# A streaming encoder layer on one core: the order of the in-projection blocks, and weight preparation without a limit on VectorE's backlog

## The chip, the cores and the metric

The kernel runs on one core of a Trainium2 chip. The metric is the device time of one execution in microseconds (us); less is better. The kernel uses TensorE (PE, with its weight loads PEld), VectorE (DVE), ScalarE (ACT), GpSimd (POOL), and the DMA queues of SyncE (SP), POOL and ACT.

## The reference, cut to what matters

One layer processes 1024 rows of a prompt and 64 rows of a running stream, 1088 in all, with 2048 features each.

```
h = rms_norm(x, norm_g)
z = h @ w_in                              # 2048 x 7296: 57 blocks of 128 columns
u, v, g_a = split(z[:, :3072], 3)         # part A
vn = layer_norm(gelu(v), ...)
out_a = gelu(u) * sgu_mix(vn) * silu(g_a)
r, k, vb, hw, ha = split(token_shift(z[:, 3072:6272]), ...)   # part B
d = w0 + tanh(hw) @ w2 ;  decay = exp(-exp(-softplus(-d) - 0.5)) ;  a = sigmoid(a0 + ha @ a2)
# per head, per row: S = S * decay - (S kk) b^T + v k^T ;  y = S r     (16 heads of 64)
out_b = (group_norm(y) * gn_g + gn_b + bonus) * silu(z[:, 6272:])
y = rms_norm(x + concat(out_a, out_b) @ w_out, final_g)
```

The outputs are y for both streams, the last states S, the last unshifted rows, and vn of the short stream.

## The kernel before, in words

**Blocks.** The in-projection is cut into 57 blocks of 128 output columns. Blocks 0 to 7 are u, 8 to 15 v, 16 to 23 the gate g_a, 24 to 31 r, 32 to 39 k, 40 to 47 vb, 48 holds hw and ha, and 49 to 56 are the gates of part B. Activations `h` and weights are each split into a high and a low part of 16 bits, and three products (high by high, high by low, low by high: `PASSES`) are added in PSUM. A block is three groups of columns (364, 364 and 360 rows of h, `MG`), each with 16 x 3 matrix products (`in_group`, L569). `h` fills the large tile `bigt` until the last block has run.

**Weights.** For each block or out-projection group a generator `wprep` (L535) takes raw weights from one tile `raw`. It squares them on ACT, sums them with a small product on PE (`total`), derives a power-of-two scale on DVE, and then splits four pieces of 512 columns: the high part on ACT, the low part on DVE (L194). After that it issues the load of the next raw weights on SP's queue. The preparation of job i + 1 is added to the planner when job i starts on PE.

**Part B by pairs.** Two heads make a pair; pair q needs k block 32 + q, vb block 40 + q, r block 24 + q, and at its end gate 49 + q. A finished k, vb or r block is written to DRAM by `z_out` (L626), a gate by `gate_out` (L635), both on SP's queue, and their u buffer is then free. `front(q)` (L825) computes decay and a, reads k, then the state and r, and then vb (`z_load`, L643), all on SP's queue, and multiplies on POOL, ACT and DVE. It then writes the tiles AR and KB in three parts; a part waits for the flags "mid", "late" and "chain" of pair q - 1. `wkv(q)` (L928) forms products of these parts, masks them on POOL (L1022), and transposes KB on PE (after which the flag ("kbfree", q) is set). It then inverts a triangular system: four DVE transposes (L1045), thirty steps of two DVE instructions (L1049 to L1056), a second set of transposes, and small products on PE. After it comes a chain of 17 steps, each of which goes from PE to DVE and back; its end stores the state `o_sp` (L1167). `front(q + 1)` is added right after the first four transposes of `wkv(q)`. `post(q)` (L1197) does the group norm, multiplies by the gate and writes the mix row block to DRAM. `a_out(i)` (L737) does the same for part A from blocks i and 16 + i, with two POOL instructions among others.

**Out-projection.** It has two halves of the contracted dimension, each with eight groups of 256 output columns. Half 0 needs mixes 0 to 6 and 8 (pair 0), half 1 the rest (`HALF`). `mix_prep(0)` (L1248) is added when block 31 is done. It waits for its mixes, computes a scale, waits for ("kbfree", 7), and then starts `mix_stage`, which reads the eight tiles back on POOL's queue. Each tile is split into two halves of 16 bits in two pieces, high part on ACT and low part on DVE (L1274). Tiles 0 and 1 go to part of `wk`. For tiles 2 to 7, `mix_place` (L1282) takes a u buffer if `room7` allows it, and else waits until the in-projection has ended and takes a place in `bigt`; such tiles are later moved to u buffers by `mix_move`. `out_first` (L1355) runs group 0 of half 0: for four row blocks at a time it first takes tiles 0 to 5, then 6 and 7.

**Buffers.** There are 13 u buffers of 128 x 1105 floats. Every in-projection block takes one, and so do most steps of `front`, `wkv`, `post` and `a_out`. `room7` (L1235) counts how many must stay free for work still to come before a mixed tile may take one.

**The planner.** The order of instructions on each engine is fixed when the program is built. `run` issues the matrix products of the blocks in the order of `order`, and after every few products calls `poll` (L155). It holds an estimated clock for each engine, and advances every generator whose due time has come. A generator is passed over while the estimated clock of DVE is ahead of PE's by more than the generator's `backlog` (ns):

```
for it in list(self.side):
    if it[0] > self.now or self.clk[DV] > self.now + it[2]:
        continue
```

The engines then run their streams on the chip in that order, and semaphores make one wait for another. DMA queues issue in order too.

Of the kernel before, what the change touches and what calls it, by code (L numbers as in the profile page):

```python
# [44 lines left out]
class Builder:  # L45
# [1188 lines left out]

    def room7(self, staging=False):  # L1235
        F = self.flags
        need = 0 if ("gb", 7) in F else 1
        if ("mix", 7) not in F:
            need += (23 not in self.gelu_buf) + (7 not in self.fbuf)
        if staging:  # L1240
            pass
        elif ("xal", 7) not in F:
            need += 4
        elif ("xfr", 7) in F and ("ysq", 7) not in F:
            need += 3
        return len(self.ufree) > need
# [242 lines left out]
    def run(self):  # L1489
        nc = self.nc  # L1490
        order = list(range(8, 16)) + [48, 32, 40, 24]
        for q in range(7):
            order += [49 + q, q, 16 + q]
            if q < 6:
                order += [33 + q, 41 + q, 25 + q]
        order += [39, 47, 31, 7, 23, 56]
        jobs = [("in", b) for b in order] + [("out", hf, g) for hf in range(2) for g in (0, 1, 2, 3, 4, 5, 7, 6)]
        self.jobs = jobs
        self.mstg = {}
        self.mixT = [{}, {}]  # L1500
        self.mixA, self.mixB = [], []
        self.minv = [None, None]
        gen = lambda i: self.wprep(jobs[i], i, jobs[i + 1] if i + 1 < len(jobs) - 2 else None)
        self.late = order[:3]
        self.raws = {}
        self.xarr = {}
        self.xf, self.xp = {}, {}
        self.load_consts()
        for j in range(2):
            self.xarr[0] = self.dma(nc.sync, self.xw[0][:, j * 1024:(j + 1) * 1024],  # L1510
                                    self.a["x"][0:128, j * 1024:(j + 1) * 1024], 1 << 19)
        self.raw_load(jobs[0])
        self.x_load(1)
        self.raw_load(jobs[1], [self.alloc(), self.alloc()])
        self.x_load(2)
        self.raw_load(jobs[2], [self.alloc(), self.alloc()])
        self.x_load(3)
        self.load_consts2()
        self.add(self.startup(), front=True)
        self.add(self.after_x())  # L1520
        plan = [(0, 0, 128), (0, 128, 128), (1, 0, 256), (0, 256, 128), (2, 0, 256), (1, 256, 128), (2, 256, 128)]
        plan += [(i, 384, 128) for i in range(3)]
        plan += [(i, t0, 128) for t0 in (512, 640) for i in range(3)]
        plan += [(i, t0, n) for i in range(3) for t0, n in ((768, 256), (1024, 64))]
        for i, t0, n in plan:
            while ("x", (t0 + n + 127) // 128 - 1) not in self.flags or ("w", jobs[i]) not in self.flags:
                self.spin()
            self.in_group(order[i], i, t0, n)
            if t0 == 1024:
                self.block_done(order[i])  # L1530
                if i == 0:
                    self.add(gen(3), backlog=2500)
        nj = len(jobs)
        for i, job in enumerate(jobs):
            if i < 3 or i > nj - 3:
                continue
            while ("w", job) not in self.flags:
                self.spin()
            if i < nj - 3:
                self.add(gen(i + 1), backlog=2500)  # L1540
            if i == nj - 6:
                self.add(self.raw_late(jobs[-2:]))
            if i == nj - 5:
                self.add(gen(nj - 2), backlog=2500)
            if job[0] == "in":
                b = job[1]
                if b == 32:
                    self.add(self.front(0), backlog=1e9)
                if b < 8:
                    self.add(self.a_load(b))  # L1550
                for t0, n in MG:
                    self.in_group(b, self.wset(i), t0, n)
                self.block_done(b)
                if b == 31:
                    self.add(self.mix_prep(0, None), backlog=1e9)
                if jobs[i + 1][0] == "out":
                    self.flags.add("inproj")
                    self.add(self.mix_move(), backlog=1e9)
            else:
                hf, gi = job[1], job[2]  # L1560
                if hf == 0 and gi == 0:
                    self.out_first(self.wset(i))
                    self.add(self.mix_prep(1, [self.wk[:, j * NT:(j + 1) * NT].bitcast(F16) for j in range(8)]))
                    continue
                if hf == 1 and gi == 0:
                    self.free(*self.mixA)
                    self.add(self.fg_load())
                if i < nj - 3:
                    self.out_group(hf, gi, self.wset(i))
                else:  # L1570
                    self.add(gen(nj - 1), backlog=2500)
                    self.out_last([(jobs[k][2], self.wset(k)) for k in range(nj - 3, nj)])
        nc.scalar.dma_start(self.a["o_sh"], self.sh[:].rearrange("p a b -> p (a b)"))
        while self.side:
            self.spin()
# [70 lines left out]
```

## Time and profile before

| | us |
|---|---|
| three runs: median (lowest to highest) | 1996.18 (1995.94 to 1999.48) |
| the profiled execution, its own time | 1999.07 |
| its span, first to last instruction | 1997.4 |
| mean granted clock of TensorE | 0.988 of full |

The profiled execution is one execution of the same program; its time lies 2.9 us above the median of the three runs. Its trace gives the start and duration of every instruction. "Busy" is time in which an engine executes; idle time is put down to what ended it. The granted clock is a share of 2.4 GHz; where it is not 1.0, part of the stretch ran at 1.2 GHz. A row of the timeline merges neighbouring instructions of the same kind ("x4").

### The profile page before, as it was taken

The numbers are of one execution on the slowest core, as the hardware profiler recorded it, in microseconds if no ns is written. First come the engines' busy times: TensorE is split into PE (matmuls) and PEld (weight loads), VectorE is DVE, ScalarE is ACT, GpSimd is POOL, SyncE is SP. The second block draws the span as 40 slices with busy tenths as digits, with TensorE's granted clock in tenths as the row PEclk, the third lists the DMA queues.
The fourth block names the chain that finished last, engine by engine and source line by source line (L and its number), as shares of the span: only waits on it lengthen the run. The fifth ranks groups of instructions, "written<-read, shape, count | busy, mean of one in ns | idle before, by whom it ended". The sixth has DMA issues, their size and how long they took to land. (4 is left out here: it accounts for less than half of the span.)

```text
span 1997.4 us, 42939 instructions
## 1 busy us (share of the span) xinstructions
PE 1929.3 (97%) x18429; PEld 1395.4 (70%) x18429; DVE 1152.4 (58%) x2557; ACT 1017.8 (51%) x1855; POOL 351.9 (18%) x360
## 2 busy tenths in 40 slices
PE   6999999999999999999999999999999789999998
PEld 6966667665766666676666666666666468899997
DVE  6574684274566557548456654753845676553444
ACT  7633334566556555654755565565473633232433
POOL 2400000330420240141033034005102400100000
PEclk9999999999999999999999999999999889999999
DMA  6221123222222312211232131221132344512114
GB/s 237 86 75 43 46 97 139 100 79 67 89 69 84 138 43 86 108 63 62 100 122 66 61 142 64 82 101 69 67 133 77 145 143 162 199 58 100 68 41 141
DMA packets 52622, 192.33 MB, mean 96 GB/s; under 512 B 6928, under 2 KB 18720, under 8 KB 42768
## 3 DMA queue, kind: packets, MB, share of 16 engines
q1 hardware_dynamic: 42064, 157.33, 22.7%
q0 software_dynamic: 6880, 22.26, 3.2%
q10 hardware_dynamic: 3488, 9.99, 1.3%
q8 instruction: 145, 2.38, 0.5%
q14 instruction: 45, 0.37, 0.1%
HBM read 140.32 MB, written 45.93 MB: 93 GB/s over the span
## 5 line engine op out<-in xcount | busy, mean ns | idle before, releaser
L245 PE MATMUL mp<-bigt,w 128*128 128x364 f16 (+3 forms) x8508 | 1330.3, 310 | 2.0 <-DVE w L194 1.1
L245 PEld LDWEIGHTS <-w 128*128 128x128 f16 x9216 | 816.8, 98 | 409.3 <-issue 4.5
L194 DVE SCALAR_TENSOR_TENSOR w<-raw,sci,w 128x512 f16<-128x512 f32 x276 | 231.7, 863 | 179.3 <-ACT w L186 178.7
L245 PEld LDWEIGHTS <-wk 128*128 128x128 f16 x2304 | 209.8, 98 | 35.8 <-ACT wk L186 3.7
L186 ACT ACTIVATE w<-raw,sci 128x512 f16<-128x512 f32 x276 | 185.9, 714 | 57.5 <-DVE sci L303 50.0
L245 PE MATMUL mp<-w,wk 128*128 128x256 f16 x1728 | 204.8, 274 | 9.5 <-DVE bigt L194 6.0
L201 POOL TENSOR_TENSOR u<-u,u 128x544 f32<-128x544 f32 (+1 forms) x112 | 152.1, 1387 | 274.1 <-DVE u L194 82.5
L186 ACT ACTIVATE w<-raw 128x2048 bf16<-128x2048 f32 (+1 forms) x70 | 131.8, 1883 | 96.2 <-PE mp L245 95.6
L186 ACT ACTIVATE wk<-bigp 128x512 f32<-128x512 f32 (+6 forms) x248 | 120.8, 511 | 69.7 <-PE bigp L245 37.3
L186 ACT ACTIVATE u<-yps 64x128 f32<-64x128 f32 x120 | 32.8, 273 | 220.9 <-DVE wk L203 220.3
L245 PE MATMUL mp<-w,u 128*128 128x256 f16 x1035 | 127.9, 273 | 0.0
L186 ACT ACTIVATE u<-mp,sc 128x364 f32<-128x364 f32 (+3 forms) x109 | 57.2, 524 | 133.9 <-PE mp L245 132.8
L194 DVE SCALAR_TENSOR_TENSOR bigt<-mp,sc,bigt 128x512 f32<-128x512 f32 (+2 forms) x83 | 53.9, 652 | 109.2 <-PE mp L245 108.9
L1131 DVE SCALAR_TENSOR_TENSOR S<-S,pc,smp 64x64 f32<-64x64 f32 x240 | 66.9, 279 | 80.0 <-PE smp L245 76.3
L186 ACT ACT_TABLE_LOAD x84 | 107.8, 1283 | 7.6 <-PE smp L245 3.2
L245 PEld LDWEIGHTS <-u 128*128 128x128 f16 x1035 | 100.6, 98 | 12.0
L186 ACT ACTIVATE u<-mp,zs 128x364 f32<-128x364 f32 (+1 forms) x75 | 42.0, 560 | 128.7 <-PE mp L245 128.4
L203 POOL TENSOR_TENSOR wk<-wk,mask 128x512 f32<-128x512 f32 (+1 forms) x80 | 85.1, 1084 | 121.0 <-ACT wk L186 117.5
L203 DVE TENSOR_TENSOR u<-u,u 128x228 f32<-128x228 f32 (+15 forms) x248 | 90.8, 367 | 8.3
L194 DVE SCALAR_TENSOR_TENSOR u<-mp,zs,u 128x363 f32<-128x363 f32 (+1 forms) x100 | 49.4, 494 | 77.2 <-ACT sht L186 52.3
L203 DVE TENSOR_TENSOR u<-bigp,u 128x512 f32<-128x512 f32 (+3 forms) x72 | 41.6, 579 | 80.8 <-PE smp L245 55.5
L223 DVE STREAM_TRANSPOSE wk<-u 32x256 f32<-32x256 f32 (+1 forms) x128 | 57.9, 453 | 45.4 <-ACT u L186 43.6
(186 smaller groups left out, 1912.0 us busy)
## 6 DMA issues: line engine op xcount, KB each, us to landing
raw<-w_in SPq DMA_DIRECT2D x54, 1024.0 KB, 4.9
raw<-w_out SPq DMA_DIRECT2D x14, 1024.0 KB, 4.9
z_d<-u SPq DMA_DIRECT2D x24, 544.0 KB, 4.1
u<-z_d SPq DMA_DIRECT2D x24, 544.0 KB, 5.0
mix_d<-u ACTq DMA_DIRECT2D x16, 544.0 KB, 3.0
o_y<-bigt SPq DMA_DIRECT2D x16, 512.0 KB, 4.1
wk<-x SPq DMA_DIRECT2D x7, 1024.0 KB, 7.9
bigt<-x POOLq DMA_DIRECT2D x7, 1024.0 KB, 9.0
```

What stands on the lines that cost most here:

```text
L186: self.nc.scalar.activation(out, in_, func, bias=bias, scale=scale, **kw)
L194: self.nc.vector.scalar_tensor_tensor(out, in0, s, in1, op0, op1)
L201: eng.tensor_tensor(out[:, c], a[:, c], b[:, c], op)
L203: (eng or self.nc.vector).tensor_tensor(out, a, b, op)
L223: self.nc.vector.transpose(out, a)
L245: self.nc.tensor.matmul(out, lhsT, rhs, start=start, stop=stop)
L1131: self.nc.vector.scalar_tensor_tensor(Sn[hp, hp], Sc[hp, hp], pc[hp, c - 1:c], pu[hp, hp], ALU.mult, ALU.add)
```

## The change

The order of the in-projection blocks is rewritten. Before, the blocks after 8 to 15, 48, 32, 40 and 24 were groups of gate 49 + q, u block q, g_a block 16 + q, then k, vb and r of pair q + 1, for q from 0 to 6 (the last group without k, vb, r), and then 39, 47, 31, 7, 23, 56. After, the first group has no gate (0, 16, 33, 41, 25), each later group q begins with gate 48 + q, the groups run on through pair 7's k, vb and r (54, 6, 22, 39, 47, 31), and the list ends with 7, 23, 55, 56. So the k, vb and r blocks of pairs 1 to 7 and all u and g_a blocks stand one place earlier, gates 49 to 54 five places later, gate 55 seven places later, and gate 56 where it was.

`room7` counts a free buffer for each of the last two gates that is neither done nor holding its buffer; before it counted one for the last gate until it was done.

The weight preparations added in the loop over jobs get a backlog limit of 1e9 ns instead of 2500, so that `poll` never passes them over for DVE's clock. The preparations of job 3 and of the last two jobs keep 2500.

```diff
     def room7(self, staging=False):
         F = self.flags
-        need = 0 if ("gb", 7) in F else 1
+        need = sum(1 for b in (6, 7) if ("gb", b) not in F and 49 + b not in self.gelu_buf)
         if ("mix", 7) not in F:
             need += (23 not in self.gelu_buf) + (7 not in self.fbuf)
...
         order = list(range(8, 16)) + [48, 32, 40, 24]
         for q in range(7):
-            order += [49 + q, q, 16 + q]
-            if q < 6:
-                order += [33 + q, 41 + q, 25 + q]
-        order += [39, 47, 31, 7, 23, 56]
+            order += [48 + q, q, 16 + q] if q else [0, 16]
+            order += [33 + q, 41 + q, 25 + q]
+        order += [7, 23, 55, 56]
...
             if i < nj - 3:
-                self.add(gen(i + 1), backlog=2500)
+                self.add(gen(i + 1), backlog=1e9)
```

## Rows read from the trace of the kernel before

**Rows 1.** The page: busy time by engine, granted clock of 40 slices, weight-splitting group.

```profile
PE 1929.3 (97%) x18429; PEld 1395.4 (70%) x18429; DVE 1152.4 (58%) x2557; ACT 1017.8 (51%) x1855; POOL 351.9 (18%) x360
...
PEclk9999999999999999999999999999999889999999
...
L194 DVE SCALAR_TENSOR_TENSOR w<-raw,sci,w 128x512 f16<-128x512 f32 x276 | 231.7, 863 | 179.3 <-ACT w L186 178.7
```

**Rows 2.** Windows: stretch, length, busy time per engine, granted clock, DMA share, GB/s.

```profile
60.00:1560.00 1500.00, 1478.22 (x13365) 999.63 (x13364) 878.29 (x2011) 812.26 (x1430) 302.95 (x293) 1.00 0.25 84
1560.00:1589.00 29.00, 23.75 (x274) 15.48 (x272) 18.91 (x13) 11.93 (x26) 13.97 (x19) 0.88 0.43 148
1589.00:1610.00 21.00, 9.39 (x49) 5.28 (x50) 18.59 (x44) 14.88 (x23) 1.67 (x3) 0.67 0.79 290
1610.00:1632.00 22.00, 18.86 (x194) 16.22 (x191) 20.65 (x48) 0.00 (x0) 0.00 (x0) 0.92 0.51 176
```

**Rows 3.** Waits of PE, 1589 to 1660: releaser, total us, times, longest us.

```profile
PE mp L245 <- DVE bigt L194: 12.7, 7, 3.1
PE mp L245 <- DVE wk L194: 2.0, 2, 1.5
PE mp L245 <- ACT wk L186: 1.6, 2, 1.1
PE smp L245 <- ACT w L186: 1.4, 1, 1.4
```

**Rows 4.** Timeline of PE: start, us, instruction, count, idle before it.

```profile
1569.93 1.12 PE L250 MATMUL bigp<-ident,wk 128*128 128x128 f32 x4 [5.19 <-ACT wk L186]
...
1589.45 0.39 PE L245 MATMUL mp<-w,wk 128*128 128x256 f16 x2 [0.51 <-ACT wk L186]
...
1618.54 1.44 PE L245 MATMUL mp<-w,wk 128*128 128x256 f16 x6 [3.14 <-DVE bigt L194]
```

**Rows 5.** Timeline of POOL: state stores, the run before 1566, first staging into bigt.

```profile
560.85 1.10 POOL L1168 DMA_DIRECT2D o_sp<-S  x2 [4.22 <-DVE wk L219]
...
1375.76 1.10 POOL L1168 DMA_DIRECT2D o_sp<-S  x2 [5.20 <-DVE S L211]
...
1556.49 2.64 POOL L201 TENSOR_TENSOR u<-u,u 128x544 f32<-128x544 f32 x2
...
1564.56 1.03 POOL L203 TENSOR_TENSOR wk<-wk,pc 128x512 f32<-128x512 f32 x1
...
1582.16 0.54 POOL L253 DMA_DIRECT2D bigt<-mix_d  x1 [0.74 <-PE mp L245]
```

**Rows 6.** Timeline of DVE: transposes of the inverse, one long split, mix splits.

```profile
420.85 3.93 DVE L223 STREAM_TRANSPOSE u<-wk 32x1024 f32<-32x1024 f32 x2
...
571.15 1.96 DVE L223 STREAM_TRANSPOSE u<-wk 32x1024 f32<-32x1024 f32 x1
...
1405.20 1.99 DVE L223 STREAM_TRANSPOSE u<-wk 32x1024 f32<-32x1024 f32 x1
...
1556.68 9.47 DVE L194 SCALAR_TENSOR_TENSOR w<-raw,sci,w 128x512 f16<-128x512 f32 x1 [0.85 <-ACT w L186]
...
1581.00 1.96 DVE L223 STREAM_TRANSPOSE u<-wk 32x1024 f32<-32x1024 f32 x1
...
1604.30 2.87 DVE L194 SCALAR_TENSOR_TENSOR bigt<-bigt,pwi 128x544 f16<-128x544 f32 x4
...
1627.32 1.97 DVE L223 STREAM_TRANSPOSE u<-u 128x1024 f32<-128x1024 f32 x1
```

**Rows 7.** Timeline of SP's DMA queue in pair 6: issue time, issue duration.

```profile
1349.48 0.32 SPq L253 DMA_DIRECT2D g_d<-u  x1
...
1351.34 0.47 SPq L253 DMA_DIRECT2D u<-z_d  x1
1361.98 0.34 SPq L253 DMA_DIRECT2D raw<-w_in  x1
1362.36 0.43 SPq L253 DMA_DIRECT2D u<-z_d  x1
```

## The prediction

> **What bounds the kernel now.** I read the page first. TensorE (PE) is busy for 97% of the span, VectorE (DVE) for 58% and ScalarE (ACT) for 51%; of the forty slices only 33 and 34 show a granted clock under nine tenths [rows 1]. So the end is set by the sum of PE's work, and a change can only give back time in which PE stands still or runs at the lower of its two clock levels (1.2 instead of 2.4 GHz). Then I asked for windows. From 60 to 1560 us PE is idle for 21.8 us of 1500. Slices 33 and 34 hold the change from in-projection to out-projection: 11.6 us idle of 21 (1589 to 1610) and 3.1 of 22 (1610 to 1632) [rows 2]. The waits of PE from 1589 to 1660 name the cause: 12.7 of 17.7 us are waits for DVE to write a `bigt` tile, 3.6 us for the `wk` tiles of the same kind [rows 3]. These are the tiles of the mixed activations that `mix_prep` scales and splits in two for the first out-projection half. In order of time, PE starts its first out-projection product at 1589.45 and meets its longest hole, 3.14 us, at 1618.54; another hole of 5.19 us stands before, at 1569.93 [rows 4].
>
> Why are these tiles late? `mix_prep` may start only when pair 7 has freed its `KB` region ("kbfree"), and the staging DMAs on POOL's queue reach the `bigt` buffers from 1582.16, six microseconds before the in-projection ends [rows 5]. At the same time DVE does pair 7's triangular inverse, which begins with the transposes at 1581.00 and is closed by those from 1627.32 on, so near 1631 [rows 6]; DVE is busy 18.6 of 21 and 20.7 of 22 us [rows 2]. The sixteen splitting instructions (2.87 us for four, so 11.5 us in all [rows 6]) queue between the steps of the inverse.
>
> **What sets when pair 7 comes.** I take the first transpose of each inverse as the mark of a pair. In the trace each inverse opens with four of these, and rows 6 show the first of pairs 0, 1, 6 and 7. From pair 0 to pair 1 it takes 571.15 - 420.85 = 150.3 us, from there to pair 6 (1405.20) 834.1 us in five steps, 166.8 us each [rows 6]. The mark of pair 1 follows the state store of pair 0's chain (`o_sp`, 560.85) by 10.3 us, that of pair 6 the store of pair 5's chain (1375.76) by 29.4 us [rows 5, 6]. So in the later pairs the work before the mark waits for something else than the chain. The DMA queue of SP shows for what: pair 6's `r` is read back at 1351.34, right behind the write of a gate (1349.48), and `v` at 1362.36, right behind a load of raw weights (1361.98) [rows 7]. The queue issues in order, and the gate's write waits until the gate's block has left PE. The recurrence is thus tied to the blocks: six blocks per pair, 166.8 / 6 = 27.8 us per block with the recurrence's work in between.
>
> **The order of blocks.** All blocks from 0 on move one place earlier, except the gates; within a group of six the order is as before. The k, v, r blocks of pairs 1 to 7, and the gate behind which `r` queues, come one block earlier. The work of PE, the copies and the DMAs are the same in number: removed 0, added 0. Pair 0 depends on blocks 48, 32, 40 and 24, which keep their places. Its successor cannot profit at once, since pair 1 came 10.3 us behind the chain already; I take its mark as unmoved, 571. Where the ties come 27.8 us earlier and the own pace is 150.3 against 166.8 us, each pair regains up to 16.5 us, so by pair 3 the recurrence is tied again, one block earlier. Pair 7's mark is then expected near 1581.00 - 27.8 = 1553, while the in-projection ends where it did, since PE's work before it hardly changes. The mixes 0 to 6 and 8 that `mix_prep` needs, and its trigger (block 31), also come one block earlier.
>
> From 1553 to 1589 DVE has 36 us. The inverse alone needs some 35 (1631 less 1581, less the 11.5 us of splitting and one weight preparation of 3.5), two weight preparations take four splits of 0.863 us each [rows 1], so 6.9, and the splitting 11.5: it does not all fit, but only the splitting is due by 1589, and `mix_prep` is not held back by DVE's queue. The other limit is room: h still occupies `bigt`, and six of eight tiles need one of 13 u buffers. `room7` now also counts gate 6 until its buffer is taken, one more than before; but pair 7's four buffers are then already taken and no longer reserved. I expect four of the six to fit early. The other two are split while PE works through the first six tiles of the first four row blocks. Waits left in 1589 to 1660: about 5 us, for `out_add` and the rest. Bounds: 0 (all 17.7 go) and 17.7 (nothing does). I take 12.7 us off.
>
> The clock: 0.67 of full over 21 us and 0.92 over 22 us are, at two levels, 13.9 and 3.5 us at half clock [rows 2]. With PE's busy share in each window (0.45 and 0.86) this is 6.2 + 3.0 = 9.2 us of busy time at half speed, 4.6 us lost. The lowered clock stands in the same windows as the holes; without holes I give back 4.0, bounds 0 and 4.6.
>
> The hole at 1569.93 comes from one DVE instruction, a weight split of 9.47 us from 1556.68 [rows 6], whose span lies under POOL's unbroken run from 1556.49 to 1565.6 (rows 5 show the first and the last of its five rows). ACT, then PE, wait behind it: 5.2 us [rows 4], and some us more for a half-clock stretch around it: 0.88 over 29 us is 7 us at half clock [rows 2]; at PE's busy share of 0.82 that would lose 2.9, but the hole lies in it, so I take 2.1. POOL's run is `a_out(7)` and pair 7's masks; both move by one block, so the meeting may recur. Bounds 0 and 7.3 us; I take the middle, 3.6, since which DVE instruction meets that run is open.
>
> **Weight preparation without the backlog limit.** Before, a step of `wprep` was emitted only when the planner saw DVE's queue under 2.5 us. Nothing is added; steps are emitted earlier. Between 1589 and 1660 PE has no row of waiting for a `w` tile from DVE [rows 3], so there is nothing to gain on PE; raw loads may leave SP earlier, by which `v` would come earlier. Against it, four splits per block can now stand ahead of recurrence steps in DVE's queue, 3.5 us per block [rows 1]. The chain steps of 1500 us cost PE at most the 21.8 us idle of that window [rows 2]. Bounds: a quarter of it goes (5 us gain) or it grows by half (11 us loss); I take 2 us loss, since PE has other products between the chain's steps to hide the rest.
>
> The page "SBUF — State Buffer" of the Trainium skill, section "Who interferes with whom", says that a DVE instruction with two SBUF inputs and a GpSimd instruction that reads SBUF block each other, and that the first holds the port for its whole instruction. The 9.47 us [rows 6] agree that they block, but span many POOL instructions, not one. By the page's rule a meeting costs one POOL instruction, about 1.3 us here (an estimate: the first row of the run is two in 2.64 us), and the hole of 5.2 us would not recur: the sum would be 4 us better, by the row it is as above.
>
> **Sum.** 12.7 + 4.0 + 3.6 - 2 = 18.3 us. The profiled execution took 1999.07 us (span 1997.4 and 1.7 around it), so 1980.8 in its terms; the runs' median is 1996.18, 2.9 us lower, and I carry that over: 1978 us. Its own range is 1967 to 1988.
>
> **Rivals.**
> (a) The recurrence is not pulled forward: something else than the blocks (free buffers, the planner's own pace) ties it. For: `r` queues behind the state load too, which waits for the chain. Against: the 29.4 us gap and the 150.3 us pace of pair 1. Then pair 7's mark stays at 1581 and the holes stay: 1996, within 1992 to 2000.
> (b) It comes earlier, but `room7` refuses the buffers until the in-projection ends. For: two gates at the end each want a buffer. Then only DVE is freed of the inverse; splitting alone takes 11.5 us, of which some 6 hide: gain 6 + 2 of clock, 1988.
> (c) Slower. Weight splits, no longer held back, meet POOL's runs: 9.47 us on DVE, 5.2 + 2.1 = 7.3 us on PE for each full meeting. For: POOL is busy 303 of 1500 us [rows 2]. Against: the trace has one such instruction. If the transition gains its 18.3 it decides from the third further meeting on (3 x 7.3 = 21.9, so 2000); if (a) holds, from the first (2003.5, with two 2010.8). I take 2006.
>
> **Chances.** Forecast 0.57, (b) 0.15, (a) 0.16, (c) 0.12. About 0.2% (4 us) is what a measurement of this kernel can tell from no change. Faster by more: the forecast, (b) but for 0.02, and 0.03 of (a): 0.73. Within: 0.15, from (a) and (b). Slower: 0.12. For the range I leave out 0.07 below (all holes gone: 17.7 + 4.6 + 7.3 is 29.6, so 1966) and 0.13 above 1998, so (c) and the end of (a).
>
> **What would show it.** Right: pair 7's first transpose near 1553 with the last in-projection product near 1585, and splitting to `u` buffers in between; waits of PE for `bigt` in the transition down from 12.7 to under 5 us; a clock above 0.9 there; `mp<-w,u` among the first out-projection products. Step two right: pair 1's mark within 5 us of 571 and pair 3 to 7 some 28 us earlier than now. The prediction is wrong if the marks do not move, if they move and the `bigt` waits stay, or if DVE shows several splits above 3 us.

## The result, and the profile after

The changed kernel took 1981.91 us (median of 4 runs, 1978.55 to 1983.83), the kernel before beside it 1996.13 (1995.94 to 1999.48). The ratio is 0.993, with a 95% interval of 0.9916 to 0.9945: 14.2 us faster. The forecast was 1978, so the direction and most of the amount came; 3.9 us are missing.

The profiled execution of the changed kernel is its lowest one: 1978.55 us, 3.4 below its median, while that of before lay 2.9 above its own. The two profiles therefore differ by 20.6 us of span, 6 more than the medians do. I read places from the profiles and amounts from the medians.

The page (the lines that answer to [rows 1]) shows the same number of instructions on PE, DVE and POOL, and no slice under nine tenths of the clock any more:

```profile
span 1976.8 us, 42947 instructions
...
PE 1920.4 (97%) x18429; PEld 1391.8 (70%) x18429; DVE 1152.3 (58%) x2557; ACT 1027.6 (52%) x1862; POOL 352.5 (18%) x360
...
PEclk9999999999999999999999999999999999999999
...
L194 DVE SCALAR_TENSOR_TENSOR w<-raw,sci,w 128x512 f16<-128x512 f32 x276 | 221.7, 827 | 158.6 <-ACT w L186 157.8
```

The windows (columns as in [rows 2]) show the change of projections at 1584 without its two bad slices. Of 1570 to 1592 PE is busy for all 22 us; 5.1 of 18 us are idle behind it:

```profile
1540.00:1570.00 30.00, 27.39 (x290) 17.13 (x289) 22.20 (x38) 16.44 (x31) 7.13 (x11) 0.94 0.53 185
1570.00:1592.00 22.00, 22.00 (x167) 16.04 (x165) 20.90 (x52) 10.87 (x18) 1.61 (x3) 1.00 0.37 125
1592.00:1610.00 18.00, 12.94 (x228) 10.67 (x227) 12.52 (x22) 4.88 (x11) 1.11 (x2) 0.91 0.72 237
```

The waits of PE from 1540 to 1660 say what is left: one wait for `bigt` of 5.1 us where [rows 3] had seven of 12.7, and none for `wk`. "Issue" is a stop for which the profile shows no cause:

```profile
PE mp L245 <- DVE bigt L194: 5.1, 1, 5.1
PE mp L245 <- issue: 2.6, 1, 2.6
PE yps L245 <- DVE S L219: 0.3, 1, 0.3
```

In PE's timeline (answering to [rows 4]) the first out-projection product stands at 1584.14, and it goes on with `u` tiles without a hole until 1594.8. The `bigt` wait is no wait for a mixed tile; the DVE rows below name the instruction.

```profile
1553.46 13.02 PE L245 MATMUL mp<-bigt,w 128*128 128x360 f16 x73 [2.61 <-issue]
...
1584.14 0.82 PE L245 MATMUL mp<-w,wk 128*128 128x256 f16 x6
1584.80 1.47 PE L245 MATMUL mp<-w,u 128*128 128x256 f16 x12
...
1590.72 4.09 PE L245 MATMUL mp<-w,u 128*128 128x256 f16 x36
1599.87 1.44 PE L245 MATMUL mp<-w,wk 128*128 128x256 f16 x6 [5.06 <-DVE bigt L194]
```

DVE's timeline (answering to [rows 6]): the marks of pairs 1, 4 and 7; one of the splits into `u` tiles before 1584; the last mixed tile, read from `bigt` and split from there into a `u` buffer after PE's first out-projection product; and at 1599.11 the instruction for which PE waits, an `out_add` (`bigt<-mp,sc,bigt`) behind the first of the two closing transposes of pair 7's inverse.

```profile
570.45 3.91 DVE L223 STREAM_TRANSPOSE u<-wk 32x1024 f32<-32x1024 f32 x2
...
1040.66 3.95 DVE L223 STREAM_TRANSPOSE u<-wk 32x1024 f32<-32x1024 f32 x2
...
1545.77 3.92 DVE L223 STREAM_TRANSPOSE u<-wk 32x1024 f32<-32x1024 f32 x2
...
1563.43 0.78 DVE L194 SCALAR_TENSOR_TENSOR u<-u,pwi,u 128x544 f16<-128x544 f32 x1 [4.48 <-ACT u L186]
...
1591.89 0.78 DVE L194 SCALAR_TENSOR_TENSOR u<-bigt,pwi,u 128x544 f16<-128x544 f32 x1
...
1597.30 1.91 DVE L223 STREAM_TRANSPOSE u<-u 128x1024 f32<-128x1024 f32 x1
1599.11 0.71 DVE L194 SCALAR_TENSOR_TENSOR bigt<-mp,sc,bigt 128x512 f32<-128x512 f32 x1
```

POOL's timeline (answering to [rows 5]): staging of mixed tiles begins at 1543.85, into `u` buffers, and only the last of the eight tiles is staged in `bigt`, at 1580.03.

```profile
1543.85 2.21 POOL L253 DMA_DIRECT2D u<-mix_d  x4
...
1580.03 0.54 POOL L253 DMA_DIRECT2D bigt<-mix_d  x1 [9.36 <-PE mp L245]
```

The SP queue in pair 6 (answering to [rows 7]): `r` is read at 1321.76 and the gate is written 12 us later, at 1333.89. `r` no longer stands behind the gate.

```profile
1321.76 0.54 SPq L253 DMA_DIRECT2D u<-z_d  x1
...
1333.89 0.32 SPq L253 DMA_DIRECT2D g_d<-u  x1
```

The marks of all pairs (first transpose of each inverse), in whole us; "order alone" is the first experiment:

| pair | 0 | 1 | 2 | 3 | 4 | 5 | 6 | 7 |
|---|---|---|---|---|---|---|---|---|
| before | 421 | 571 | 737 | 905 | 1072 | 1238 | 1405 | 1581 |
| changed | 422 | 570 | 732 | 895 | 1041 | 1202 | 1367 | 1546 |
| order alone | 420 | 566 | 727 | 880 | 1043 | 1206 | 1377 | 1551 |
| gate third | 424 | 569 | 738 | 909 | 1077 | 1237 | 1402 | 1568 |
| gate two pairs later, limit kept | 420 | 570 | 722 | 887 | 1052 | 1218 | 1384 | 1537 |

A ledger of the two profiles. PE ends the in-projection 4.8 us earlier in the changed kernel (1588.9 before, 1584.1 now): its idle time from 60 us on is 26.2 against 27.0, and it has 6.8 us at half clock against 20.5. In the 75 us behind that point PE is idle for 5.6 us against 17.6, and has 3.4 us at half clock against 17.1. From that point to the end the difference is 15.8 us. Of these 12.0 are idle time, and I put the remaining 3.8 down to the clock.

### The profile page after: what moved, and what is told of

It reads as the page before. It is cut to its first block, busy times and chain, and to the rows that moved or that the text cites. A ratio compares the mean times of both kernels' runs of the same rounds, so it can differ in the third digit from the quotient of the medians.

```text
span 1976.8 us, 42947 instructions
## 1 busy us (share of the span) xinstructions
PE 1920.4 (97%) x18429; PEld 1391.8 (70%) x18429; DVE 1152.3 (58%) x2557; ACT 1027.6 (52%) x1862; POOL 352.5 (18%) x360
## 5 line engine op out<-in xcount | busy, mean ns | idle before, releaser
L194 DVE SCALAR_TENSOR_TENSOR w<-raw,sci,w 128x512 f16<-128x512 f32 x276 | 221.7, 827 | 158.6 <-ACT w L186 157.8
L201 POOL TENSOR_TENSOR u<-u,u 128x544 f32<-128x544 f32 (+1 forms) x112 | 156.5, 1424 | 256.5 <-DVE u L194 105.4
L245 PE MATMUL mp<-w,u 128*128 128x256 f16 x1152 | 141.2, 273 | 0.0
L245 PEld LDWEIGHTS <-u 128*128 128x128 f16 x1152 | 112.1, 98 | 13.5
L203 DVE TENSOR_TENSOR u<-u,u 128x108 f32<-128x108 f32 (+15 forms) x248 | 91.4, 368 | 8.3
```

The lines of the kernel that those rows point to most:

```text
L194: self.nc.vector.scalar_tensor_tensor(out, in0, s, in1, op0, op1)
L201: eng.tensor_tensor(out[:, c], a[:, c], b[:, c], op)
L203: (eng or self.nc.vector).tensor_tensor(out, a, b, op)
L245: self.nc.tensor.matmul(out, lhsT, rhs, start=start, stop=stop)
```

## Experiments

Each ratio is to the kernel before, run beside it on the same chip (1996.13 us beside the first row of the changed kernel; 1995.2, 1995.46 and 1994.66 in the sessions of the others). "Out start" is the first out-projection product, "lead" the time from pair 7's mark to it, "idle" PE's idle time in the 75 us after the last in-projection product, all in us and from the profiled execution.

| kernel | median | ratio [95%] | out start | lead | idle |
|---|---|---|---|---|---|
| before | | 1 | 1589.4 | 8 | 17.6 |
| changed | 1981.91 | 0.993 [0.9916, 0.9945] | 1584.1 | 38 | 5.6 |
| changed, again | 1981.86 | 0.9931 [0.9915, 0.9947] | 1587.8 | 39 | 5.6 |
| order alone | 1976.12 | 0.9908 [0.9894, 0.9922] | 1580.8 | 30 | 9.1 |
| order alone, again | 1976.83 | 0.9916 [0.9901, 0.993] | 1582.7 | 30 | 5.8 |
| order alone, old `room7` | 1976.53 | 0.9903 [0.9886, 0.992] | 1585.9 | 30 | 4.6 |
| no limit alone | 1993.7 | 0.9994 [0.9986, 1.0003] | 1583.5 | 8 | 19.1 |
| no early split | 1997.56 | 1.0012 [1.0001, 1.0024] | 1587.1 | 37 | 16.0 |
| no limit, in-projection | 1979.29 | 0.9932 [0.9917, 0.9947] | 1586.0 | 39 | 4.4 |
| no limit, out-projection | 1979.52 | 0.9931 [0.9916, 0.9946] | 1585.7 | 30 | 8.0 |
| gate third | 1985.45 | 0.9956 [0.9943, 0.9968] | 1577.1 | 9 | 16.2 |
| `a_out(7)` on DVE | 1979.62 | 0.9921 [0.9905, 0.9937] | 1577.5 | 33 | 12.5 |
| gate two pairs later | 1974.05 | 0.9894 [0.9879, 0.9908] | 1573.7 | 38 | 6.4 |
| the same, limit kept, two `yns` | 1975.3 | 0.9895 [0.9876, 0.9914] | 1575.5 | 38 | 8.9 |

### The two parts apart

Order alone: the changed kernel with the old limit.

```diff
-                self.add(gen(i + 1), backlog=1e9)
+                self.add(gen(i + 1), backlog=2500)
```

> The new order and the new room7, with the old limit of 2500 on weight preparation. Theory (the order does it: pair 7 comes one block earlier and the mixes are split before the in-projection ends): 1980 to 1985 us, pair 7's first transpose within 10 us of 1546, PE idle in the 75 us after the first out-projection product under 7 us. Rival (the missing limit does it, by raw loads that leave SP's queue earlier): 1993 to 2000 us, transition idle near 17 us.

No limit alone: the kernel before with the new limit.

```diff
-                self.add(gen(i + 1), backlog=2500)
+                self.add(gen(i + 1), backlog=1e9)
```

> The old order and the old room7, with weight preparation unlimited. Theory: no change beyond a reshuffled planner, 1993 to 2000 us, pair 7's first transpose at 1575 to 1585, transition idle 14 to 20 us. Rival (the missing limit does it): 1980 to 1986 us. If a mere reshuffle moves the time by some 5 us, this run shows that too.

The order carries all of the gain (0.9908), and more than the whole change has: its 1976.12 us lie under the range that I expected, though 9.1 us of idle time stay where I expected under 7. The limit alone does nothing that can be measured (0.9994, its interval holds 1): its lead stays at 8 us and its idle time at 19.1.

### Is it the earlier splitting, or the earlier recurrence?

The changed kernel, but `mix_place` gives no `u` buffer before the in-projection has ended. Tiles 2 to 7 go to `bigt` as in the worst case of the kernel before; the recurrence stays early (mark 1550).

```diff
-            if self.room7():
-                self.mixA.append(self.alloc())
-                return self.U(self.mixA[-1]).bitcast(F16)
```

> The changed kernel, but mixed tiles 2 to 7 may not take u buffers before the in-projection has ended (only tiles 0 and 1 are split before, the rest as in the old kernel in bigt). Theory (the split before the end of the in-projection is what fills the holes): 8 to 13 us of PE idle come back right after the first out-projection product, 1989 to 1996 us, although pair 7's mark stays near 1546. Rival (what counts is that DVE has finished more of pair 7's inverse by then): idle grows by under 4 us, 1982 to 1986 us.

The whole gain was gone: 1.0012 [1.0001, 1.0024]. With the mark 31 us earlier than before and the inverse's closing transposes from 1587.7 on, PE still meets holes behind the in-projection. First the waits of PE from 1580 to 1660, then two rows of PE's timeline, at the start of the out-projection and at the longest hole:

```profile
PE mp L245 <- DVE bigt L194: 8.2, 4, 3.4
PE yps L245 <- ACT wk L186: 2.5, 1, 2.5
PE yps L245 <- DVE S L219: 1.6, 1, 1.6
PE mp L245 <- ACT bigt L186: 1.6, 2, 0.9
```

```profile
1587.11 0.82 PE L245 MATMUL mp<-w,wk 128*128 128x256 f16 x6
...
1624.84 1.46 PE L245 MATMUL mp<-w,wk 128*128 128x256 f16 x6 [3.41 <-DVE bigt L194]
```

Of the 16.0 us of idle time, 6.4 are waits for tiles that are split only now, the last of them at 1598.77. The longest hole is an `out_add` (DVE at 1624.03) that waits for the load of x, which ACT issues only at 1616.39, and 4.7 us are waits of pair 7's chain. That these follow from the late splits too, on which ACT and DVE are at work, is likely but not shown.

From the out start to the end of the span this kernel takes 408.9 us, the kernel before 407.9, and the two profiles of the changed kernel 392.6 and 394.3. So behind the out start the earlier recurrence earns nothing by itself; it is the condition under which the splits can be done early. Whether it earns something ahead of the out start this run does not tell, since it also has the missing limit, whose cost the next section measures.

### What the missing limit costs

The changed kernel and order alone were each run again, and the limit was lifted for one kind of weight at a time (diffs against the changed kernel; the repetition of it has none).

> The changed kernel itself, on the same chip as the next three, to be set beside the kernel with the order alone (1976 us when it ran). Theory (the missing backlog limit costs a few us, as forecast with 2): 1979 to 1984 us. Rival (the two do not differ, only the day did): 1974 to 1978 us.

> The order alone once more, on the same chip as the three others, as their base. Theory: 1975 to 1978 us, as when it first ran. Rival (its lead of 5.5 us over the changed kernel was the day's): 1979 to 1984 us.

```diff
-                self.add(gen(i + 1), backlog=1e9)
+                self.add(gen(i + 1), backlog=1e9 if jobs[i + 1][0] == "in" else 2500)
```

> The new order and room7, with weight preparation unlimited for the in-projection blocks and limited to 2500 for the out-projection groups. The changed kernel took 1981.9 us and the order alone 1976.1. Theory (the lost 5 to 6 us lie before the out-projection starts, where the changed kernel's profiles reach it 3 to 7 us later): 1980 to 1984 us. Rival (they lie in the transition, where weight splits stand before mix splits and out_add): 1975 to 1978 us.

```diff
-                self.add(gen(i + 1), backlog=1e9)
+                self.add(gen(i + 1), backlog=2500 if jobs[i + 1][0] == "in" else 1e9)
```

> The reverse: limited to 2500 for the in-projection blocks, unlimited for the out-projection groups. Theory (loss before the out-projection): 1975 to 1978 us, the out-projection starting near 1581. Rival (loss in the transition): 1980 to 1984 us, with waits for bigt above 9 us after the start of the out-projection.

Both repeat: 1981.9 twice with the change, 1976.1 and 1976.8 with the order alone. Taking off the limit costs about 5.4 us on top of the new order. The intervals of single pairs overlap; what I rest on is the same sign in every comparison, and all runs taken together: ten of the changed kernel lie between 1978.40 and 1984.12, nine of the order alone between 1975.05 and 1979.67. The two kernels with the limit lifted for one kind of weight lie between (1979.3 and 1979.5), and in both cases between the range of the theory and that of the rival. Their intervals overlap with those of both ends, so it is not shown that each kind carries half of the cost. Of the in-projection's part, 2.0 us can be seen as idle time before the out start: 26.2, 27.0 and 26.5 us in the three profiles with it, 25.0, 23.6, 24.9 and 24.8 in four without it. Which waits these are, and where the rest goes, the profiles do not show; one execution of a kernel differs from the next by as much.

### Does the new `room7` matter?

Order alone with the old line.

```diff
-        need = sum(1 for b in (6, 7) if ("gb", b) not in F and 49 + b not in self.gelu_buf)
+        need = 0 if ("gb", 7) in F else 1
```

> The order alone with the old room7 (one buffer kept for the last gate until that gate is done, none for gate 6). Theory (the new count only keeps the planner from giving away a gate's buffer and moves little): within 3 us of the order alone, 1974 to 1979 us. Rival (the new count is what lets tiles into u buffers early): the transition idle rises above 10 us, 1984 us or more.

No difference can be measured: 1976.53 against 1976.12 and 1976.83.

### Is the recurrence tied by the gate's write?

The order alone, with the gate third in its group instead of first. The k, v and r blocks keep their places; the u and g_a blocks move up by one.

```diff
-            order += [48 + q, q, 16 + q] if q else [0, 16]
+            order += [q, 16 + q, 48 + q] if q else [0, 16]
```

> The order alone, but within each group the gate stands after u and g_a instead of before them, so that r's read is no longer queued behind the gate's write on SP. Theory (that write ties the recurrence to the blocks): r is read right behind the first chain step of the pair before, and the marks of pairs 4 to 6, 1043, 1206 and 1377 with the gate first, come 10 us or more earlier. Rival (raw weight loads, buffers or the planner's pace tie it as well): marks within 8 us of those. The time hangs on pair 7 alone and should stay within 1973 to 1980 us in both.

SP's queue in pair 5 of this kernel: `r` (one of the two `u<-z_d` at 1193.89) is read well before the gate's write at 1209.08. DVE's row gives its mark, 1237.01, against 1206.28 in order alone, where the gate's write comes 1.7 us before `r` (1150.52 and 1152.24):

```profile
1193.89 1.37 SPq L253 DMA_DIRECT2D u<-z_d  x2
1209.08 0.32 SPq L253 DMA_DIRECT2D g_d<-u  x1
```

```profile
1237.01 3.90 DVE L223 STREAM_TRANSPOSE u<-wk 32x1024 f32<-32x1024 f32 x2
```

```profile
1150.52 0.32 SPq L253 DMA_DIRECT2D g_d<-u  x1
1150.89 1.25 SPq L887 DMA_DIRECT2D st<-state  x2
1152.24 0.53 SPq L253 DMA_DIRECT2D u<-z_d  x1
```

If `r` behind the gate's write were the tie, this kernel would be the free one; it is the late one. Its marks from pair 2 on are those of before, within 5 us up to pair 6, and its idle time is 16.2. So the gate's write in front of `r` in the queue is not what ties the marks. A shift of the gate by two blocks, with the u and g_a blocks one place earlier, is enough to lose the lead; which of these moves does it, and by which way (the buffer that the gate holds, `post` of the pair, the planner's due times), no run tells.

The time, 1985.45, missed the 1973 to 1980 that I expected, yet it is still 9.2 us under the kernel before. This gain is not the early splitting: from the out start to the end the kernel takes 406.2 us, against 407.9 before. It reaches the out start at 1577.1 instead of 1589.4, with 22.1 us of idle time from 60 us on instead of 27.5, and no weight split over 2 us stands in its trace. So an order can also gain ahead of the transition, without what this change was made for.

### Going on: gates two pairs later

If one pair later helps, two may help more. The first kernel of this kind, which has no limit, does not give the right rows of y for the short stream: one tile of the chain (`yns`) is written again before the late `post` has read it. The second gives `yns` two tiles and keeps the limit; space for it comes from three small tiles that share others.

```diff
-            order += [48 + q, q, 16 + q] if q else [0, 16]
+            order += [47 + q, q, 16 + q] if q > 1 else [q, 16 + q]
             order += [33 + q, 41 + q, 25 + q]
-        order += [7, 23, 55, 56]
+        order += [7, 23, 54, 55, 56]
```

> Each pair's gate two pairs later (gates 5, 6 and 7 at the end), so k, v and r come one more block earlier; room7 counts three gates. Theory: marks from pair 4 or 5 on another 15 to 28 us earlier, pair 7 near 1520 to 1530; the out-projection finds all its tiles and DVE free of the inverse, so the 5.1 us hole after the first four row blocks goes as well: 1973 to 1980 us. Rival (the recurrence's own pace binds now, since its pairs took 146 to 165 us): pair 7's mark within 8 us of 1546 and the time within 3 us of the changed kernel.

```diff
-        self.yns = t([128, 128], F32, "yns")
+        self.yns = [t([128, 128], F32, f"yns{i}") for i in range(2)]
...
-            yd = self.yns[HP[q % 2]] if c == 16 else Y[c % 2 * 64:c % 2 * 64 + 64, c // 2]
+            yd = self.yns[q // 2 % 2][HP[q % 2]] if c == 16 else Y[c % 2 * 64:c % 2 * 64 + 64, c // 2]
```

> Gates two pairs later, with the old backlog limit, and the short stream's chain output held in two tiles instead of one (a gate that late lets pair q + 2 reach its first chain step before pair q's output has been used; three small tables share memory to make room). Theory: 1971 to 1977 us, pair 7's mark between 1525 and 1545 and a hole at the second four row blocks under 3 us. Rival (the recurrence's own pace binds, nothing more to win): the time of the order alone, 1975 to 1979 us.

Each has to be set beside the kernel with the same limit. Without a limit it took 1974.05, against 1981.9 for the changed kernel, and the intervals do not meet (0.9894 [0.9879, 0.9908] and 0.993 [0.9916, 0.9945]): 7.8 us faster. With the limit it took 1975.3, against 1976.1 to 1976.8 for the order alone: not told apart from it. Both reach the out start early (1573.7 and 1575.5), with 18.1 and 16.9 us of idle time from 60 us on. Pair 7's mark is 1536 and 1537, not the 1520 to 1530 of the first theory, and marks 4 to 6 are later than in the changed kernel. Something else seems to hold the recurrence by then. SP's queue in pair 6 of the second kernel suggests what: the state load and both `u<-z_d` follow a load of raw weights. I did not test it.

```profile
1330.42 0.33 SPq L253 DMA_DIRECT2D raw<-w_in  x1
1330.81 1.11 SPq L887 DMA_DIRECT2D st<-state  x2
1331.96 1.06 SPq L253 DMA_DIRECT2D u<-z_d  x2
```

### A hole taken away that gave nothing

Order alone still has the long weight split (shown in the last section), and behind it a PE hole of 5.2 us. Here the POOL product of `a_out(7)`, part of the run that it meets, is done by DVE.

```diff
-        yield self.tt(self.U(gu), self.U(gu), self.U(f), ALU.mult, eng=nc.gpsimd)
+        yield self.tt(self.U(gu), self.U(gu), self.U(f), ALU.mult, eng=nc.gpsimd if i < 7 else None)
```

> The order alone (old limit), and for mix 7 the first product of part A on VectorE instead of POOL, so that POOL's run before pair 7's masks loses 2.6 us of two instructions. Theory (the 9.5 us weight split waits for POOL's unbroken run, and PE then for 5.2 us): no DVE instruction above 3 us after 1500, the 5.2 us hole before the out-projection gone, 1969 to 1973 us. Rival (the split is slow because of something else, or PE's hole is filled by another wait): the long split stays or a hole of 3 us or more takes its place, 1974 to 1979 us.

The hole went (the longest split is 3.77 us) and the out start came at 1577.5, 3.3 us earlier than in order alone. The time did not follow: 1979.62. PE's waits from 1500 to 1670, its timeline, and DVE's at the end of the wait:

```profile
PE mp L245 <- DVE bigt L194: 11.8, 2, 11.2
```

```profile
1577.52 0.82 PE L245 MATMUL mp<-w,wk 128*128 128x256 f16 x6
...
1599.80 1.44 PE L245 MATMUL mp<-w,wk 128*128 128x256 f16 x6 [11.19 <-DVE bigt L194]
```

```profile
1597.30 1.90 DVE L223 STREAM_TRANSPOSE u<-u 128x1024 f32<-128x1024 f32 x1
1599.06 0.68 DVE L194 SCALAR_TENSOR_TENSOR bigt<-mp,sc,bigt 128x512 f32<-128x512 f32 x1
```

PE reached the transition earlier and waited for the same `out_add`, which came no earlier: 1599.06 here, 1599.11 in the changed kernel, 1597.93 and 1596.52 in the two profiles of the order alone. The gain before the transition was given back in it. Two things set the time of this add. Here, as in the changed kernel, it stands behind closing transposes of the inverse on DVE. In the order alone those come only after it (1602.30), and it waits for a DMA, the load of x into the sum to which it adds:

```profile
1597.93 0.75 DVE L194 SCALAR_TENSOR_TENSOR bigt<-mp,sc,bigt 128x512 f32<-128x512 f32 x1 [3.50 <-DMA bigt<-x]
```

ACT issues that load behind a weight preparation, at 1589.11 in the order alone and, though PE is ahead, at 1590.89 here:

```profile
1590.89 0.42 ACTq L253 DMA_DIRECT2D bigt<-x  x1
```

It landed 5.6 us later, at 1596.45, so a DVE free of the inverse would have moved the add by 2.6 us at most.

## Why the prediction was right, point by point

**The recurrence is pulled forward: right, and further than expected.** Pair 1's mark stayed (570 against 571) and pair 7's came at 1546, where 1553 was forecast; rival (a) is out. It was caught up later than I wrote: pair 3 had 10 us, pair 4 had 31. The cause that I gave is not borne out. I read from [rows 7] that `r` waits behind the gate's write. With the gate third, `r` is ahead of that write and the marks fall back. The place of the gate sets the pace, but not by that queue.

**The splits fit early: right, and better than counted.** I expected four of the six tiles to fit early; five were split into `u` buffers before the out start, and the sixth, staged in `bigt`, was split from there into a `u` buffer by 1592.7. Rival (b) is out. The run without early splits shows that in the changed kernel this step carries the gain behind the out start (408.9 us without it, 392.6 and 394.3 with it).

**12.7 us of waits: 12.0.** The idle time behind the in-projection fell from 17.6 to 5.6, where about 5 was expected to stay, "for `out_add` and the rest". Nearly all of it is one hole of 5.06 us, and it is `out_add`. One reading behind the term was wrong. I took all 12.7 us of `bigt` waits in [rows 3] for waits for mixed tiles. The hole at 1618.54, the longest, ended with an `out_add` already in the kernel before, by DVE's row:

```profile
1617.74 0.74 DVE L194 SCALAR_TENSOR_TENSOR bigt<-mp,sc,bigt 128x512 f32<-128x512 f32 x1
```

So did two later ones, and the three together are 6.0 us. Mixed tiles account for 6.7 us in `bigt` and 3.6 in `wk`. These 10.3 us are what the early splits removed; the waits for `out_add` went from 6.0 only to 5.1. The size came out right because I had left about 5 us for `out_add`.

**The clock, 4.0: about 3.8** behind the in-projection, by what the idle time leaves over (17.1 to 3.4 us at half clock).

**The hole at 1569.93, 3.6: not earned as such.** The 9.47 us split is gone from the changed kernel, and came back in all three runs of the order alone. But PE's idle time up to the end of the in-projection fell only from 27.0 to 26.2; among other things a new hole of 2.6 us, with no shown cause, stands at 1550.85. The rest of the 4.8 us that the profile shows there I put down to half-clock time, of which the profiled execution of before had much (20.5 us; the kernel before with the limit off had 6.8). I don't count it.

**No backlog limit, 2 us lost: the mis-sized term.** It costs about 5.4 us with the new order, inside the bounds of -11 to +5 that the text gave but far from the value taken. With the old order it costs nothing that can be measured (0.9994). The order alone gained 19.1 us (1995.2 less 1976.1), close to the 20.3 of the other three terms, which is luck in part: the 9.46 us split and the 5.2 us hole behind it stand in the order alone, so the 3.6 us counted for that hole were not earned where they were forecast. What the limit took beyond 2 (3.4 us) is most of the 3.9 us by which the forecast missed. I had argued that PE finds other products between the chain's steps. That is not shown; nor is rival (c)'s mechanism, since no split over 2.60 us is in the changed kernel's trace.

## What to carry to other kernels

When PE meets holes at a change of stage, look for the last thing that must be ready there, and ask what in the order of the whole program sets how early it can start; here moving gates that nobody needs soon gave 19 us with the same products. Test the parts of a change apart even when the sum is a gain: here one part took back a quarter of it. A hole removed ahead of a due point counts only as far as everything that the due point waits for comes earlier as well (here `out_add`, which needs both DVE, busy with the inverse, and the load of x).

## What the runs showed of the hardware

The same meeting of DVE's weight splits with POOL's run took two quite different forms. In order alone, one split took 9.46 us from 1527.15 (a usual one there takes 0.75), under eight POOL instructions that begin 0.2 us ahead of it and follow each other to 1536.05. DVE, then POOL:

```profile
1527.15 9.46 DVE L194 SCALAR_TENSOR_TENSOR w<-raw,sci,w 128x512 f16<-128x512 f32 x1 [0.84 <-ACT w L186]
```

```profile
1526.96 2.64 POOL L201 TENSOR_TENSOR u<-u,u 128x544 f32<-128x544 f32 x2
1529.56 2.27 POOL L203 TENSOR_TENSOR wk<-wk,mask 128x512 f32<-128x512 f32 x2
...
1535.02 1.03 POOL L203 TENSOR_TENSOR wk<-wk,pc 128x512 f32<-128x512 f32 x1
```

In the changed kernel the splits come some 2 us into such a run, and both engines go on, each somewhat slower: the four splits take 1.01, 1.56, 1.64 and 1.18 us, and two mask products on POOL 2.71 instead of 2.27. DVE, then POOL:

```profile
1533.37 1.01 DVE L194 SCALAR_TENSOR_TENSOR w<-raw,sci,w 128x512 f16<-128x512 f32 x1 [2.29 <-ACT w L186]
1535.49 1.56 DVE L194 SCALAR_TENSOR_TENSOR w<-raw,sci,w 128x512 f16<-128x512 f32 x1 [1.12 <-ACT w L186]
```

```profile
1531.19 2.63 POOL L201 TENSOR_TENSOR u<-u,u 128x544 f32<-128x544 f32 x2
1533.79 2.71 POOL L203 TENSOR_TENSOR wk<-wk,mask 128x512 f32<-128x512 f32 x2
```

Six kernels have the first form, at 9.45 to 9.47 us: before, no limit alone, the three runs of the order alone, and the one that lifts the limit for the out-projection only. The four that lift it for the in-projection under the new order have the second (the changed kernel twice, the one without early splits, and that part alone). The page "SBUF — State Buffer" of the Trainium skill, section "SBUF: two separate sides", has a DVE instruction with two SBUF inputs and a POOL instruction that reads SBUF block each other for the whole instruction of whoever came first. The second form keeps within that (0.9 us lost at most by a split, less than one POOL instruction); the first, eight POOL instructions long, does not. What decides between them was not tested.
